# Four pads move every activation tile to one place, 64 bytes short of the weights by 256, in a two-layer decoder trunk

## The chip, the core and the metric

The kernel runs on one core of a Trainium2 chip. The metric is the device time of one execution in microseconds (us). Beside the times of several runs there is one profiled execution, from which the pages and rows below come; its span goes from the first to the last instruction.

## What is computed

Two layers of a decoder with 256 tokens and a width of 1024, all in float32. Each layer adds a token mixer and then a conv-gated MLP to the residual, each behind an rmsnorm, and a last rmsnorm ends it:

```
for i in range(DEPTH):                       # DEPTH = 2
    hn = rms_norm(h, norm_mix[i])
    if kind == 0:   mix = moba_mixer(hn, ...)   # layer 0: causal attention, 16 heads of 64
    elif kind == 1: mix = mla_mixer(hn, ...)    # layer 1: low-rank q and kv latents, shared rotary key
    h = h + mix
    f = conv_ffn(rms_norm(h, norm_ffn[i]), w_gate, conv_w, conv_b, w_up, w_down)
    h = h + f
return rms_norm(h, norm_final)

def conv_ffn(xn, ...):
    g = xn @ w_gate                          # 1024 -> 2816
    gc = conv_b + sum(conv_w[j] * shifted(g, j) for j in range(3))
    return (gelu(gc) * (xn @ w_up)) @ w_down # 2816 -> 1024
```

With 256 tokens the block choice of the first mixer leaves plain causal attention.

## The kernel before

Activations lie with features on the partitions and the 256 tokens along them, as 8 chunks of 128 features (`h`, `zh`, `zl`: 128 x 8 x 256). All weights come as a stream of units in the order in which they are used: `load_unit` sends one DMA of up to 576 KB into `raw` (5 buffers), ScalarE casts it to the rounded format fp32r into `whi` (line 172), and VectorE forms the rest `wlo = raw - whi` (line 173); `whi` and `wlo` have 9 buffers each. Activations are split in the same way, into `zh` and `zl` (lines 184 and 185), `oh` and `ol`, `ch` and `cl`, `hh` and `hl`. A product is then three matmuls, lines 177 to 179 in `mm3`: high by high, high by low, low by high, into one accumulator in PSUM.

In a matmul one operand is loaded into the array first (LDWEIGHTS, PEld in the profile) and the other moves through it (MATMUL, PE). In the profile's `acc<-zh,whi` the first name moves, the second is loaded. The load for the next matmul runs beside the current matmul.

The program goes through these stages, in the order of the code and with no scheduler in between:

1. Layer 0, first head group: Q, K and V from `zh`, `zl` (about 6 to 27 us of the span). Per chunk of features 12 matmuls of Q and K, in which `zh` and `zl` move, alternate with 6 of V, in which weights move and `zh`, `zl` are loaded.
2. Attention of layer 0: head by head, with the products of the next group, and later the output projection (`oh`, `ol` move), filled in between (to about 127 us).
3. The MLP of layer 0, `ffn`: for 22 chunks the gate and the up product (`zh`, `zl` move) and the gate's elementwise work; then the down product in `to_layer1` (`hh`, `hl` move), to about 313 us.
4. Layer 1: the latents (`ch`, `cl`), attention and output projection, to about 410 us; the MLP's gate and up products, to about 534 us; the down product in `to_out`, in which the weights move in pieces of 512 columns and `hh`, `hl` are loaded, to about 598 us; the last norm and the stores.

Tiles are laid one after the other within a pool, and pools one after the other: constants, `rawp`, `wp`, `act` (`h`, `zh`, `zl` and small ones), `sm`, and then one pool that is opened and closed per stage (`at0`, `ff0`, `at1`, `ff1`). All large tiles are whole multiples of 256 bytes per partition, so the first tile of a pool sets the place of all large tiles of it, counted by 256 bytes. Three pads do that in the kernel before: 8 columns (32 bytes) ahead of `act`, 16 columns (64 bytes) in `at0` and `at1`, none in the MLPs.

Of the kernel before, what the change touches and what calls it, by code (L numbers as in the profile page):

```python
# [10 lines left out]
F32 = mybir.dt.float32  # L11
# [5 lines left out]
P = 128  # L17
# [102 lines left out]
def trunk(ctx: ExitStack, tc: tile.TileContext, xT, scalars, gfin, wstream, consts_in, out):  # L120
# [4 lines left out]
    act = ctx.enter_context(tc.tile_pool(name="act", bufs=1))  # L125
    sm = ctx.enter_context(tc.tile_pool(name="sm", bufs=4))
    ps = ctx.enter_context(tc.tile_pool(name="ps", bufs=1, space=PSUM))
    act.tile([P, 8], F32, name="pad")


    zf = rawp.tile([P, UW], F32, name="raw")[:, :S]
# [25 lines left out]
    def load_unit(cuts=2, pieces=1, mid=None):  # L157
        u = state["u"]
        state["u"] += 1
        n = UCOLS[u]  # L160
        raw = rawp.tile([P, UW], F32, name="raw")
        hi = wp.tile([P, UW], F32R, name="whi")
        lo = wp.tile([P, UW], F32R, name="wlo")
        for i in range(pieces):
            a, b = n * i // pieces, n * (i + 1) // pieces
            src = bass.AP(tensor=wstream.tensor, offset=wstream.offset + UOFF[u] + a, ap=[[n, P], [1, b - a]])
            nc.sync.dma_start(raw[:, a:b], src)
            if mid is not None and i == 0:
                mid()
        for i in range(cuts):  # L170
            a, b = n * i // cuts, n * (i + 1) // cuts
            nc.scalar.copy(hi[:, a:b], raw[:, a:b])  # L172
            nc.vector.tensor_sub(lo[:, a:b], raw[:, a:b], hi[:, a:b].bitcast(F32))  # L173
        return hi, lo

    def mm3(o, lh, ll, rh, rl, first, last):
        nc.tensor.matmul(o, lh, rh, start=first, stop=False, skip_group_check=True)  # L177
        nc.tensor.matmul(o, ll, rh, start=False, stop=False, skip_group_check=True)  # L178
        nc.tensor.matmul(o, lh, rl, start=False, stop=last, skip_group_check=True)  # L179
# [31 lines left out]
    def rstd(pc, n):  # L211
        ms = sm.tile([P, NT], F32, name="ms")
        nc.vector.tensor_scalar(ms, pc, 1.0 / n, EPS, op0=ALU.mult, op1=ALU.add)  # L213
        r = sm.tile([P, NT], F32, name="r")
        nc.gpsimd.tensor_tensor(r, ms, mhalf.to_broadcast([P, NT]), op=ALU.pow)  # L215
        return r
# [20 lines left out]
    def rows_sb(r):  # L237
        R = act.tile([P, S], F32, name="R", bufs=2)
        nc.scalar.copy(R, rows(r))
        return R  # L240
# [137 lines left out]

    def ffn(layer, zh, zl, ss):
        with tc.tile_pool(name=f"ff{layer}", bufs=1) as fp:  # L380
            hh = fp.tile([P, FC, S], F32R, name="hh")
            hl = fp.tile([P, FC, S], F32R, name="hl")
            st = {}

            def products(f0, j, pg, pu):
                ug, uu = load_unit(), load_unit()
                runs = ((0, KD),) if f0 + j else ((0, KD - 2), (KD - 2, KD))
                for a, b in runs:
                    for k in range(a, b):
                        for (wh, wl), dst in ((ug, pg), (uu, pu)):  # L390
                            c = slice(k * P, (k + 1) * P)
                            mm3(dst[:, j], wh[:, c], wl[:, c], zh[:, k], zl[:, k], k == 0, k == KD - 1)

            def gate(f0, pg, pu):
                Rb = st["R"][:, None, :].to_broadcast([P, 2, S])
                gm = fp.tile([P, 2, S], F32, name="gm", bufs=2)
                nc.vector.tensor_tensor(gm, pg, Rb, op=ALU.mult)  # L397
                gc = fp.tile([P, 2, S], F32, name="gc", bufs=2)
                for j in range(2):
                    w = cv[:, layer, f0 + j]  # L400
                    nc.scalar.activation(gc[:, j], gm[:, j], AF.Identity, scale=w[:, 2:3], bias=w[:, 3:4])  # L401
                    nc.vector.scalar_tensor_tensor(gc[:, j, 1:], gm[:, j, :S - 1], w[:, 1:2], gc[:, j, 1:],
                                                   op0=ALU.mult, op1=ALU.add)
                    nc.vector.scalar_tensor_tensor(gc[:, j, 2:], gm[:, j, :S - 2], w[:, 0:1], gc[:, j, 2:],
                                                   op0=ALU.mult, op1=ALU.add)
                nc.scalar.activation(gc, gc, AF.Gelu)  # L406
                nc.gpsimd.tensor_tensor(gc, gc, Rb, op=ALU.mult)  # L407
                nc.vector.tensor_tensor(gm, pu, gc, op=ALU.mult)  # L408
                nc.scalar.copy(hh[:, f0:f0 + 2], gm)  # L409
                nc.vector.tensor_sub(hl[:, f0:f0 + 2], gm, hh[:, f0:f0 + 2].bitcast(F32))  # L410

            late = None
            for f0 in range(0, FC, 2):
                pg = ps.tile([P, 2, S], F32, name="acc", bufs=4)
                pu = ps.tile([P, 2, S], F32, name="acc", bufs=4)
                products(f0, 0, pg, pu)
                if late:
                    st["R"] = rows_sb(r)
                    gate(*late)
                    late = None  # L420
                products(f0, 1, pg, pu)
                if f0 == 0:
                    r = rstd(ss.columns(), D)
                    late = (f0, pg, pu)
                else:
                    gate(f0, pg, pu)
            (to_layer1 if layer == 0 else to_out)(fp, hh, hl)
# [87 lines left out]

    zh, zl = new_z()
    with tc.tile_pool(name="at0", bufs=1) as ap:
        ap.tile([P, 16], F32, name="pad")
        oh = ap.tile([P, KD, S], F32R, name="oh")
        ol = ap.tile([P, KD, S], F32R, name="ol")  # L520
        ropeR = ap.tile([P, 2, S], F32, name="ropeR")
# [124 lines left out]
        finish(accs, us, [(oh[:, k], ol[:, k]) for k in (KD - 2, KD - 1)], GF, zh, zl, ss)  # L646

    ffn(0, zh, zl, ss)


    zh, zl = nxt["z"]
    with tc.tile_pool(name="at1", bufs=1) as ap:
        ap.tile([P, 16], F32, name="pad")
        ch = ap.tile([P, CQ + CKV, S], F32R, name="ch")
        cl = ap.tile([P, CQ + CKV, S], F32R, name="cl")
        kTs = [ap.tile([P, HG, S], F32, name=f"kT{i}") for i in range(2)]
# [151 lines left out]
        finish(accs, us, [(oh[:, k], ol[:, k]) for k in (KD - 2, KD - 1)], GF + KD, zh, zl, ss)  # L808

    ffn(1, zh, zl, ss)  # L810


# [25 lines left out]
```

## Time and profile before

| | us |
|---|---|
| median of 3 runs | 606.88 (606.06 to 608.16) |
| the profiled execution | 607.92 |
| its span | 606.1 |
| TensorE busy | 591.7 |
| VectorE busy | 435.2 |
| ScalarE busy | 355.6 |
| GpSimd busy | 63.2 |

Matmuls are pipelined, and the end of one is modelled, so that matmuls overlap in the list and a busy TensorE is not a TensorE at its peak. What can be read exactly is when each one starts. In an unbroken run the distance from start to start is the pace of the engine; it is taken over many matmuls, since starts are shown to 10 ns.

### The profile page before, as it was taken

To read this page: it belongs to the slowest core of one execution; us is meant where nothing else is said; L and a number is where in the kernel's file an instruction comes from. 1 tells how busy PE (TensorE), PEld (TensorE's weight loads), DVE (VectorE), ACT (ScalarE), POOL (GpSimd) and SP (SyncE) were. 2 spreads that over 40 slices of the span, in tenths; PEclk is the share of its full clock that TensorE was granted. 3 is DMA by queue.
4 is the path that set the end of the run, shared out by engine and by line. 5 is a ranking of instruction groups with operands and counts; after the bars stand their busy time and mean duration, and the time that the engine had idled before them with its cause. 6 is when DMAs were issued, how large, how long until landed. Compare 5 with 4: busy or idle time off the path is not lost.

```text
span 606.1 us, 12092 instructions
## 1 busy us (share of the span) xinstructions
PE 591.7 (98%) x4631; PEld 562.9 (93%) x4631; DVE 435.2 (72%) x948; ACT 355.6 (59%) x760; POOL 63.2 (10%) x55
## 2 busy tenths in 40 slices
PE   8999899999999999999999999999999999999994
PEld 8997798999999999999999888999999999988883
DVE  6899878695877777764488889658778777784403
ACT  7687766575655565543366677546666566573302
POOL 1110210000210110200002210000020100110001
PEclk9999999999999999999999999999999999999998
DMA  8746564436466656675637323155466656666101
GB/s 279 279 140 229 166 198 145 142 127 214 146 203 186 199 172 204 186 228 166 187 116 258 127 70 107 70 171 177 140 209 199 195 172 204 200 186 198 40 0 70
DMA packets 30074, 101.62 MB, mean 168 GB/s; under 512 B 3488, under 2 KB 4848, under 8 KB 30016
## 3 DMA queue, kind: packets, MB, share of 16 engines
q1 hardware_dynamic: 29744, 100.24, 51.3%
q8 instruction: 36, 0.59, 0.4%
q0 software_dynamic: 128, 0.35, 0.2%
q10 hardware_dynamic: 144, 0.26, 0.1%
q14 instruction: 22, 0.18, 0.1%
HBM read 99.79 MB, written 1.05 MB: 166 GB/s over the span
## 4 chain that ended last, share of the span: by engine, by line
PE 73%; issue 13%; DVE 6%; DMA 4%; ACT 3%; POOL 1%; SPq 0%; POOLq 0%; DVEq 0%; ACTq 0%
PE acc L177 19%; PE acc L178 18%; PE acc L179 18%; PE sc L274 3%; DMA raw<-in_wstream 3%; PE tr L314 2%; DVE wlo L173 2%; PE sc L179 2%; PE tr L179 2%; PE tr L178 2%; PE sc L178 2%; PE sc L177 2%; PE tr L177 2%; PE sc L300 1%; ACT whi L172 1%
## 5 line engine op out<-in xcount | busy, mean ns | idle before, releaser
L173 DVE TENSOR_TENSOR wlo<-raw,whi 128x512 fp32r<-128x512 f32 (+1 forms) x371 | 240.1, 687 | 61.3 <-ACT whi L172 61.2
L172 ACT CAST whi<-raw 128x512 fp32r<-128x512 f32 (+1 forms) x371 | 210.3, 617 | 119.9 <-PE acc L179 60.1
L177 PE MATMUL acc<-zh,whi 128*128 128x256 f32 x880 | 248.6, 283 | 0.3 <-ACT whi L172 0.3
L178 PE MATMUL acc<-zh,wlo 128*128 128x256 f32 x880 | 246.6, 280 | 0.0
L179 PE MATMUL acc<-zl,whi 128*128 128x256 f32 x880 | 245.8, 280 | 0.0
L177 PEld LDWEIGHTS acc<-zh,whi 128*128 128x128 f32 x880 | 165.6, 189 | 2.9 <-issue 2.0
L178 PEld LDWEIGHTS acc<-zh,wlo 128*128 128x128 f32 x880 | 165.8, 188 | 0.3 <-DVE wlo L173 0.2
L179 PEld LDWEIGHTS acc<-zl,whi 128*128 128x128 f32 x880 | 165.5, 188 | 0.0
L407 POOL TENSOR_TENSOR gc<-gc,R 128x512 f32<-128x512 f32 x22 | 34.9, 1585 | 200.3 <-ACT gc L406 200.3
L409 ACT CAST hh<-gm 128x512 fp32r<-128x512 f32 x22 | 13.7, 621 | 44.1 <-DVE gm L408 44.1
L177 PE MATMUL acc<-oh,whi 128*128 128x256 f32 x128 | 37.8, 295 | 0.0
L178 PE MATMUL acc<-oh,wlo 128*128 128x256 f32 x128 | 36.2, 283 | 0.0
L179 PE MATMUL acc<-ol,whi 128*128 128x256 f32 x128 | 36.0, 281 | 0.0
L288 ACT ACTIVATE pb<-sb,nm 128x128 f32<-128x128 f32 x64 | 28.5, 446 | 7.8 <-DVE nm L285 7.7
L408 DVE TENSOR_TENSOR gm<-acc,gc 128x512 f32<-128x512 f32 x22 | 15.2, 691 | 23.8 <-POOL gc L407 23.8
L215 POOL TENSOR_TENSOR r<-ms,mhalf 128x2 f32<-128x2 f32 x6 | 7.0, 1168 | 190.5 <-DVE ms L213 190.5
L177 PEld LDWEIGHTS acc<-oh,whi 128*128 128x128 f32 x128 | 24.1, 188 | 1.4 <-issue 1.4
L401 ACT ACTIVATE gc<-gm,sc_in 128x256 f32<-128x256 f32 x44 | 24.0, 592 | 1.9 <-DVE gm L397 1.8
L178 PE MATMUL tr<-hh,wlo 128*128 128x256 f32 x88 | 24.6, 280 | 0.0
L177 PE MATMUL sc<-hh,whi 128*128 128x256 f32 x88 | 24.6, 280 | 0.0
L179 PE MATMUL sc<-hl,whi 128*128 128x256 f32 x88 | 24.6, 280 | 0.0
L179 PE MATMUL tr<-hl,whi 128*128 128x256 f32 x88 | 24.6, 280 | 0.0
(150 smaller groups left out, 992.8 us busy)
## 6 DMA issues: line engine op xcount, KB each, us to landing
raw<-in_wstream SPq DMA_DIRECT2D x175, 512.0 KB, 4.2
raw<-in_wstream SPq DMA_DIRECT2D x13, 256.0 KB, 4.7
raw<-in_wstream SPq DMA_DIRECT2D x4, 576.0 KB, 3.8
h<-in_xT SPq DMA_DIRECT2D x8, 128.0 KB, 4.6
gl<-in_gfin SPq DMA_DIRECT2D x1, 512.0 KB, 3.7
out<-hn SPq DMA_DIRECT2D x1, 512.0 KB, 2.6
ropeR<-in_consts POOLq DMA_DIRECT2D x1, 256.0 KB, 4.1
out<-hn ACTq DMA_DIRECT2D x1, 256.0 KB, 3.7
```

Of the source, the lines that this page charges most:

```text
L172: nc.scalar.copy(hi[:, a:b], raw[:, a:b])
L173: nc.vector.tensor_sub(lo[:, a:b], raw[:, a:b], hi[:, a:b].bitcast(F32))
L177: nc.tensor.matmul(o, lh, rh, start=first, stop=False, skip_group_check=True)
L178: nc.tensor.matmul(o, ll, rh, start=False, stop=False, skip_group_check=True)
L179: nc.tensor.matmul(o, lh, rl, start=False, stop=last, skip_group_check=True)
L274: nc.tensor.matmul(o[:, a:b], self.qT(n, t), self.kT(n, b - a), start=True, stop=True)
L288: nc.scalar.activation(pb[:, a:b], sb[:, a:b], AF.Exp, scale=-1.0, bias=nm[:, t:t + 1], accum_out=rs[:, t:t + 1])
L314: nc.tensor.matmul(o[j * HD:(j + 1) * HD, t * P:], self.v(n, t), pT[j][:, a:b], start=t == 0, stop=t == NT - 1)
L401: nc.scalar.activation(gc[:, j], gm[:, j], AF.Identity, scale=w[:, 2:3], bias=w[:, 3:4])
L407: nc.gpsimd.tensor_tensor(gc, gc, Rb, op=ALU.mult)
L408: nc.vector.tensor_tensor(gm, pu, gc, op=ALU.mult)
L409: nc.scalar.copy(hh[:, f0:f0 + 2], gm)
```

## The change

```diff
@@ trunk: pool act
-    act.tile([P, 8], F32, name="pad")
+    act.tile([P, 48], F32, name="pad")
@@ ffn
         with tc.tile_pool(name=f"ff{layer}", bufs=1) as fp:
+            fp.tile([P, 32], F32, name="pad")
             hh = fp.tile([P, FC, S], F32R, name="hh")
@@ pools at0 and at1
-        ap.tile([P, 16], F32, name="pad")
+        ap.tile([P, 32], F32, name="pad")
```

Nothing reads or writes a pad. In the two built programs the instructions, their order on every engine and their waits are the same; what differs is where tiles lie. Bytes into a partition, by 256, with the distance of the activation from the weights in brackets:

| tiles | before | after |
|---|---|---|
| `raw`, `whi`, `wlo` (all buffers) | 32 | 32 |
| `h`, `zh`, `zl`, `R`, `sq`, `ssacc` | 64 (+32) | 224 (-64) |
| `oh`, `ol`, `ch`, `cl`, `qT`, `kT`, `v`, `pn`, `pT` | 0 (-32) | 224 (-64) |
| `hh`, `hl`, `gm`, `gc`, `gl`, `hn` | 192 (+160, or -96) | 224 (-64) |
| constants (`ident`, the mask) | 0 | 0 |

Where the weights move and an activation is loaded, the distance has the other sign.

## Rows read from the trace of the kernel before

**Rows 1.** Busy time of each engine in five stretches, granted clock, DMA share
```profile
core 0: us, PE busy (x) PEld busy (x) DVE busy (x) ACT busy (x) POOL busy (x), PEclk, DMA share, GB/s
30.00:128.00 98.00, 93.92 (x778) 85.56 (x778) 80.57 (x217) 69.64 (x182) 10.80 (x7) 1.00 0.51 167
128.00:251.00 123.00, 123.00 (x1053) 122.84 (x1053) 94.68 (x171) 72.61 (x134) 16.48 (x11) 1.00 0.58 182
251.00:313.00 62.00, 62.00 (x531) 62.00 (x530) 34.85 (x59) 29.09 (x54) 2.03 (x1) 1.00 0.62 191
...
412.00:534.00 122.00, 122.00 (x1045) 121.84 (x1044) 93.84 (x169) 71.74 (x132) 16.46 (x11) 1.00 0.59 186
534.00:599.00 65.00, 64.41 (x290) 51.96 (x288) 27.05 (x46) 22.53 (x43) 2.84 (x3) 1.00 0.30 95
```
**Rows 2.** What TensorE's matmuls waited for: us in total, times, longest
```profile
PE tr L314 <- DVE pT L305: 4.1, 4, 2.2
```
**Rows 3.** Timeline of PE, layer 0 gate and up: first and last of 854 spacings
```profile
151.56 0.28 PE L177 MATMUL acc<-zh,whi 128*128 128x256 f32 x1
...
251.19 0.28 PE L179 MATMUL acc<-zl,whi 128*128 128x256 f32 x1
```
**Rows 4.** Timeline of PE, layer 0 down product: first and last of 524 spacings
```profile
251.66 0.28 PE L177 MATMUL sc<-hh,whi 128*128 128x256 f32 x1
...
313.14 0.28 PE L179 MATMUL tr<-hl,whi 128*128 128x256 f32 x1
```
**Rows 5.** Timeline of PE, layer 1 output projection: first and last of 64 spacings
```profile
402.43 0.28 PE L178 MATMUL acc<-oh,wlo 128*128 128x256 f32 x1
...
410.00 0.28 PE L179 MATMUL acc<-ol,whi 128*128 128x256 f32 x1
```
**Rows 6.** Timeline of PE, V in layer 0: first and last of 21 spacings
```profile
92.54 0.28 PE L178 MATMUL acc<-whi,zl 128*128 128x256 f32 x1
...
95.03 0.28 PE L178 MATMUL acc<-whi,zl 128*128 128x256 f32 x1
```
**Rows 7.** Timeline of PE, layer 1 down product: first and last of 222 spacings
```profile
545.98 0.39 PE L178 MATMUL tr<-whi,hl 128*128 128x512 f32 x1
...
597.78 0.39 PE L178 MATMUL tr<-whi,hl 128*128 128x512 f32 x1
```
**Rows 8.** Timeline of PE, first group of layer 0: first and last of 72 spacings
```profile
11.84 0.28 PE L179 MATMUL acc<-zl,whi 128*128 128x256 f32 x1
...
20.28 0.28 PE L179 MATMUL acc<-zl,whi 128*128 128x256 f32 x1
```
**Rows 9.** Groups of matmuls, one line of three: xcount | busy, mean ns | idle
```profile
L177 PE MATMUL acc<-zh,whi 128*128 128x256 f32 x880 | 248.6, 283 | 0.3 <-ACT whi L172 0.3
L177 PE MATMUL acc<-oh,whi 128*128 128x256 f32 x128 | 37.8, 295 | 0.0
L177 PE MATMUL sc<-hh,whi 128*128 128x256 f32 x88 | 24.6, 280 | 0.0
...
L177 PE MATMUL acc<-whi,zh 128*128 128x256 f32 x64 | 18.7, 293 | 0.0
L177 PE MATMUL sc<-whi,hh 128*128 128x512 f32 x44 | 17.4, 395 | 0.0
```
**Rows 10.** Casts and subtractions with operands at 32 and at 192, all shapes alike
```profile
L173 DVE TENSOR_TENSOR wlo<-raw,whi 128x512 fp32r<-128x512 f32 (+1 forms) x371 | 240.1, 687 | 61.3 <-ACT whi L172 61.2
L172 ACT CAST whi<-raw 128x512 fp32r<-128x512 f32 (+1 forms) x371 | 210.3, 617 | 119.9 <-PE acc L179 60.1
...
L409 ACT CAST hh<-gm 128x512 fp32r<-128x512 f32 x22 | 13.7, 621 | 44.1 <-DVE gm L408 44.1
L410 DVE TENSOR_TENSOR hl<-gm,hh 128x512 fp32r<-128x512 f32 x22 | 15.2, 691 | 11.1 <-ACT hh L409 11.0
```

More of the change, by code (lines that the diff above doesn't have):

```diff
@@ L652, in trunk @@
     with tc.tile_pool(name="at1", bufs=1) as ap:
-        ap.tile([P, 16], F32, name="pad")
+        ap.tile([P, 32], F32, name="pad")
         ch = ap.tile([P, CQ + CKV, S], F32R, name="ch")
```

## The prediction

> **What bounds the kernel now.** The windows by stage come first [rows 1]. From 128 to 251 us and from 412 to 534 us (the gate and up products of the two MLPs) and from 251 to 313 us (the down product of layer 0) TensorE is busy for the whole of each stretch, at a granted clock of 1.00; in the down product of layer 1 for 64.41 of 65 us. In the attention of layer 0 it is still busy for 93.92 of 98 us. VectorE and ScalarE are at 94.68 and 72.61 of 123 us in the same stretch, the DMA at 0.58. The list of waits says the same from the other side: the longest thing TensorE's matmuls waited for is 4.1 us in total, in the attention [rows 2]. So a nanosecond on each product is paid on the path nearly everywhere, and that is the only place where an edit of addresses can be worth much: no instruction, no order and no wait changes.
>
> The question is therefore what sets the pace of one product. All large products are split in three matmuls (lines 177 to 179) and stand back to back, so the pace is the time between two starts, read from the first and the last of a long unbroken run:
> - zh and zl move over weights: 854 spacings from 151.56 to 251.19 us, 116.66 ns [rows 3]. zh and zl lie 32 bytes above the weights by 256: distance +32.
> - hh and hl move over weights: 524 spacings from 251.66 to 313.14 us, 117.33 ns [rows 4]; distance 192 - 32 = 160, or -96.
> - oh and ol move over weights: 64 spacings from 402.43 to 410.00 us, 118.28 ns [rows 5]; distance 0 - 32 = -32.
> - weights move over zh and zl (V of layer 0): 21 spacings from 92.54 to 95.03 us, 118.57 ns, with 10 ns of rounding in 2490 [rows 6]; distance 32 - 64 = -32.
> - weights of 512 columns move over hh and hl: 222 spacings from 545.98 to 597.78 us, 233.33 ns, or 116.67 per 256 columns [rows 7]; distance 32 - 192 = -160, or +96.
>
> Groups 5 and 6 have nothing in common but the distance: another operand moves, in another layer, over other buffers, and the pace is the same. Groups 3 and 5 have all in common but the distance, and differ by 1.62 ns. I take it from this that the distance between what moves and what is loaded, by 256 bytes, sets part of the pace. There is one more point. Where the first group goes from Q and K to V or back, one matmul moves while a weight at its own place is loaded, distance 0. From 11.84 to 20.28 us lie 72 spacings [rows 8]: 44 at +32, 20 at -32 and 8 such. 8440 - 44 x 116.66 - 20 x 118.28 leaves 941 ns, or 117.7 for one; rounding makes that uncertain by about 1 ns.
>
> **The change, part by part.** The weights stay where they are. The pads move h, zh, zl, oh, ol, ch, cl, hh and hl to 224 by 256, so where activations move the distance becomes -64, and where weights move +64. Neither is in the trace, so each is bounded by its neighbours.
>
> *Distance -64.* The nearest rows are -96 with 117.33 [rows 4] and -32 with 118.28 [rows 5]. A straight line between them gives 117.81; the parabola that also takes the point at 0 with 117.7 [rows 8] has its top between them and gives about 118.2. I take 118.0. Counts: the zh and zl groups have three times 880 matmuls, 2640; hh and hl as moving operand three times 88, in sc and in tr each, 528; oh and ol three times 128, 384 [rows 9].
> - zh, zl: 2640 x (118.0 - 116.66) = +3.54 us.
> - hh, hl in layer 0: 528 x (118.0 - 117.33) = +0.35 us.
> - oh, ol: 384 x (118.0 - 118.28) = -0.11 us.
>
> *Distance +64.* The neighbours are +32 with 116.66 [rows 3] and +96 with 116.67 [rows 7]; both ends agree, so I take 116.67.
> - V of layer 0, three times 64 matmuls [rows 9]: 192 x (116.67 - 118.28) = -0.31 us.
> - Down product of layer 1, 44 in each of six groups [rows 9]: 264 x 0 = 0.
>
> The products of the latents in layer 1 (14 of three matmuls in each of four groups by the loops, 168) go from +32 to +64 or from -32 to -64; at the differences above that is under 0.1 us in all. The attention's own matmuls have both operands among the activations, which move together: 0.
>
> *Other engines.* ScalarE and VectorE work on tiles at other places. With all operands at 32 a cast of 512 columns takes 617 ns and a subtraction 687; with all at 192 the same take 621 and 691 [rows 10]. That is 4 ns either way, under work of TensorE that fills the stretch, so 0. The one pair whose distance changes is gc and R in POOL's product (from 128 to 0); POOL is busy 16.48 of 123 us [rows 1], and the two PSUM pairs behind it cover it. The DMA that lands h now writes to 224 instead of 64. Every transfer of weights lands at 32 already, so a place off 64 bytes is no hindrance that shows: I count 0, and bound it by 0.3 us either way, for the eight loads of x and the stores at the end, which nothing covers.
>
> *Sum:* 3.54 + 0.35 - 0.11 - 0.31 = +3.5 us. It is made against the profiled execution: 607.92 us with a span of 606.1, where the 1.8 us around the span stay. The median before is 606.88, 1.04 below the profiled one, and a change of pace shifts both alike: 606.9 + 3.5 = 610.4 us. With the straight line's 117.81 the sum is 3.04 + 0.25 - 0.18 - 0.31 = +2.8, and with 118.28 for all of it 4.28 + 0.50 - 0.31 = +4.5: 609.7 to 611.4. Of the 2640, some 500 lie in the attention and the latents, where a slower product could hide in a wait; 4.08 us of idle time in 98 [rows 1] say that few do, and if all did, 0.7 us would go.
>
> The rows show that the same matmul takes 116.66 or 118.28 ns by where its operands lie. The Trainium skill, page "TensorE: Matmul & The Clock Gate", section "Step-by-step: what each phase is for", says that TensorE has two independent read ports to SBUF, one for the moving operand and one for the weight load, so that loading the next weights takes nothing from the running matmul. By that rule the place of a tile could not matter, and the sum would be 0 instead of +3.5. The trace speaks against it in rows 3 and 5, as long as it is the distance that makes them differ; if it is something else in those stages, the rule holds, and its result is the second rival.
>
> **The rivals.** *Faster: -64 is better than anything in the trace.* All five long runs have a distance that is an odd multiple of 32 bytes; -64 is a multiple of 64, and if the loss comes where two reads are out of step within a piece of 64 bytes, the neighbours say nothing. For it: no run shows such a distance for long. Against it: the eight overlaps at distance 0, also a multiple of 64, came to 117.7, in the middle of the others. Price: as far below the best pace seen as the best is below the worst, 1.6 ns, gives 115.0: 2640 x -1.66 - 528 x 2.33 - 384 x 3.28 - 0.31 = -4.4 - 1.2 - 1.3 - 0.3 = -7.2, or 599.7 us. It decides as soon as the pace at -64 is below about 116.5. Chance 0.26.
>
> *No change.* Either the place has no part in the pace (606.9 us), or -64 is as good as +32: then zh and zl stay, hh and oh gain 528 x 0.67 + 384 x 1.62 = 1.0 us and V 0.3, 605.6 us. For the first: the stages differ in more than the distance, in how they go round PSUM. Against it: groups 5 and 6. Chance 0.20.
>
> *Slower than the worst pace seen.* -64 is the top of the curve, and it is higher than both neighbours: at 119.0 it is 6.18 + 0.88 + 0.28 - 0.31 = +7.0, or 613.9 us. For it: the point at 0 is lower than the one at -32, so a top lies somewhere between -96 and 0. Chance 0.08.
>
> **How the numbers follow.** The forecast, 609.7 to 611.4 with 610.4 in the middle, has 0.46. This kernel's runs tell from no change what is more than about 0.3%, or 1.8 us: the limits are 605.1 and 608.7. Slower is the forecast and the last rival, 0.54; within 0.3% is the second, 0.20; faster is the first, 0.26. The range leaves out the half of the first rival that lies furthest down and most of the last: 601 to 612.5.
>
> **What would show it.** In the profile after, the run from about 151 us should have its 854 spacings at 117.8 to 118.3 ns instead of 116.66, hh at the same pace instead of 117.33, oh at the same pace instead of 118.28, V and the down product of layer 1 at 116.67 per 256 columns. All products of one direction should have one pace, since all have one distance. The stretches of the two gate and up products should each grow by about 1.4 us, and TensorE should be as busy in them as before. I am wrong if the paces by stage stay as they are (then the distance is not the cause), or if the pace at -64 lies outside of its two neighbours.

## The result and the profile after

| us | before | after |
|---|---|---|
| median | 607.41 of 4 runs (606.06 to 608.16) | 598.81 of 4 runs (596.47 to 603.31) |
| profiled execution, its span | 607.92, 606.1 | 603.31, 601.5 |

The ratio of the times is 0.988, with an interval from 0.984 to 0.991. The change makes the kernel faster, by about 1.2%, where the prediction said 3.5 us slower. The times of after also lie over 6.8 us, those of before over 2.1. Ratios and intervals, here and below, leave out executions more than 1.5% above the quickest of their kernel, which takes the slowest 3 of 7 out of again and 4 of 10 out of shift64, while the medians are of all executions.

Busy time by stretch, after; the columns are those of [rows 1]:
```profile
128.00:251.00 123.00, 123.00 (x1045) 122.84 (x1044) 93.69 (x169) 71.64 (x132) 16.46 (x11) 1.00 0.58 184
...
412.00:534.00 122.00, 122.00 (x1057) 121.31 (x1056) 96.33 (x175) 74.53 (x138) 16.43 (x11) 1.00 0.61 192
```
TensorE is busy without a gap in both gate and up stretches, as before, at a granted clock of 1.00. But the profile has 1045 matmuls in the first stretch, where it had 1053, and 1057 in the second, where it had 1045: one layer became slower and the other quicker.

Timeline of PE, after: first and last of the 854 spacings in layer 0, the same in layer 1, and first and last of the 222 spacings of 512 columns (columns: start, length, engine, line, operation, out<-moving,loaded):
```profile
150.08 0.28 PE L177 MATMUL acc<-zh,whi 128*128 128x256 f32 x1
...
250.66 0.28 PE L179 MATMUL acc<-zl,whi 128*128 128x256 f32 x1
...
434.03 0.28 PE L177 MATMUL acc<-zh,whi 128*128 128x256 f32 x1
...
530.82 0.28 PE L179 MATMUL acc<-zl,whi 128*128 128x256 f32 x1
...
542.32 0.39 PE L178 MATMUL tr<-whi,hl 128*128 128x512 f32 x1
...
593.13 0.39 PE L178 MATMUL tr<-whi,hl 128*128 128x512 f32 x1
```
Layer 0: 100.58 us over 854 is 117.78 ns. Layer 1: 96.79 over 854 is 113.33. Both runs have the same operands in the same places at the same distance, -64; [rows 3] had 116.66. The down product of layer 1 went from 233.33 [rows 7] to 228.89 ns. Every other unbroken run of 37 spacings or more at -64 in this trace has one of the same two paces. (A list of starts lacks a record here and there, so spacings are counted from the program.) So there is a slow one, 117.78, close to the 118.0 of the forecast, and a quick one, 113.33, which no row of before showed.

Of the 4.6 us of span, layer 1's gate and up run gives 2.85 and the 512-wide run 0.99; layer 0's run takes 0.95 more than [rows 3], the down product of layer 0 0.2 more than [rows 4]. The rest, some 1.9 us, comes from the attention and the shorter runs.

The other engines did not move (groups of after, as [rows 10]; hh and hl at their new place took 622 and 691 ns):
```profile
L173 DVE TENSOR_TENSOR wlo<-raw,whi 128x512 fp32r<-128x512 f32 x363 | 234.5, 685 | 60.1 <-ACT whi L172 60.0
L172 ACT CAST whi<-raw 128x512 fp32r<-128x512 f32 x363 | 205.4, 617 | 116.0 <-PE acc L179 58.1 <-PE tr L179 25.7 <-PE tr L178 16.5
```

### The profile page after: what moved, and what is told of

Read it like the earlier page. It is cut to its first block, busy times and chain, and to the rows that moved or that the text cites. A ratio compares the mean times of both kernels' runs of the same rounds, so it can differ in the third digit from the quotient of the medians.

```text
span 601.5 us, 12092 instructions
## 1 busy us (share of the span) xinstructions
PE 586.3 (97%) x4631; PEld 558.5 (93%) x4631; DVE 435.8 (72%) x948; ACT 356.1 (59%) x760; POOL 61.3 (10%) x55
## 4 chain that ended last, share of the span: by engine, by line
PE 75%; issue 12%; DVE 5%; ACT 2%; DMA 2%; POOL 2%; SPq 0%; POOLq 0%; DVEq 0%; ACTq 0%
PE acc L177 19%; PE acc L178 19%; PE acc L179 19%; PE sc L274 3%; DMA raw<-in_wstream 2%; PE tr L314 2%; PE tr L177 2%; PE sc L177 2%; PE sc L179 2%; PE tr L179 2%; PE tr L178 2%; PE sc L178 2%; PE sc L300 1%; DVE wlo L173 1%; DVE rt L531 1%
## 5 line engine op out<-in xcount | busy, mean ns | idle before, releaser
L178 PE MATMUL sc<-hh,wlo 128*128 128x256 f32 x88 | 24.7, 281 | 0.0
L177 PE MATMUL tr<-hh,whi 128*128 128x256 f32 x88 | 24.7, 281 | 0.0
```

## The experiments

Theory *distance*: the distance between the moving and the loaded operand by 256 bytes alone sets the pace, and -64 simply is a good value. Rivals: the place in memory counts and not the distance; other engines' accesses count; or something of the stage counts. A second question came with the result: what picks between the two paces at -64?

**again.** The changed kernel once more, without an edit, in more runs.

> The changed kernel once more, unchanged. In its first profile every long run of products kept one of two paces, 113.33 or 117.78 ns from start to start, and never a third (layer 0 gate and up 117.79 over 1454 spacings, layer 1 gate and up 113.33 over 854). Theory A, two lockings at distance -64, picked anew at each start: the same two paces and no other, but in some runs of products swapped against the first profile; times of single executions spread over several us, between about 594 (all long runs at 113.33) and 608 (all at 117.78). Theory B, the pace belongs to the place in the program (layer 1 is quick, layer 0 slow): every run of products keeps the pace of the first profile, and times differ by under 2 us.

Median 601.87 us of 7 runs: 596.87, 597.63, 600.51, 601.87, 606.43, 606.79, 607.22; ratio 0.990 (0.986 to 0.994), and 0.991 by the medians of all. Timeline of PE in the execution of 596.87: first and last of layer 0's gate and up run, its down product, layer 1's gate and up run:
```profile
150.18 0.28 PE L177 MATMUL acc<-zh,whi 128*128 128x256 f32 x1
...
246.97 0.28 PE L179 MATMUL acc<-zl,whi 128*128 128x256 f32 x1
...
247.42 0.28 PE L177 MATMUL sc<-hh,whi 128*128 128x256 f32 x1
...
306.81 0.28 PE L179 MATMUL tr<-hl,whi 128*128 128x256 f32 x1
...
427.59 0.28 PE L177 MATMUL acc<-zh,whi 128*128 128x256 f32 x1
...
524.38 0.28 PE L179 MATMUL acc<-zl,whi 128*128 128x256 f32 x1
```
854, 524 and 854 spacings, all of 113.33 ns. So one kernel has both paces in the same run of products, in different executions. In layer 0 the run goes over into the down product and the latents without a break, and all of it keeps one pace: (854 + 524 + 68) x 4.45 = 6.4 us; in layer 1 it is 854 x 4.45 = 3.8 us. Neither, one or both slow gives four times, 596.9 and 3.8, 6.4 and 10.2 us more: 596.9, 600.7, 603.3 and 607.1. The times of after and again lie near these, and each profiled execution agrees: after, with layer 0 slow alone, took 603.31 us, this one, with neither, 596.87.

**d0, d128, d_p64.** All activations at distance 0, at 128 and at +64, by the lengths of the same pads alone.

> All activations at distance 0 from the weights by 256 (no pad in act, 32 columns in the others, everything at 32). Theory A with 'multiples of 64 can lock at 113.33': two paces again, 113.33 and a slower one, time 594 to 608 us. Theory C, -64 alone is special and 0 is the mean of its neighbours: one pace of about 117.7 everywhere, about 609 to 611 us.

> All activations 128 bytes from the weights by 256, as far as can be. Theory A with 'any multiple of 64': 113.33 among the paces, 594 to 608 us. Theory C: between its neighbours +96 (116.67) and -96 (117.33), about 117.0, 606 to 608 us. If two reads at half the period never meet, below 113.33 everywhere, under 592 us.

> All activations 64 bytes above the weights by 256 (act pad 16 columns, the others 32): the mirror of the change. Theory A: two paces, 113.33 and 117.78, where activations move, and the same two where weights move (now at -64); 594 to 608 us. Theory C (-64 alone): where activations move one pace near that at +32, 116.7, about 605 us; the down product of layer 1, now at -64, at 229 ns per 512 columns or more.

| kernel | us (range) | ratio (interval) | zh, hh in layer 0, ns | 512 columns, ns |
|---|---|---|---|---|
| d0 | 613.89 (612.92 to 614.54) | 1.010 (1.008 to 1.012) | 120.0 | 226.77 |
| d128 | 611.51 (611.23 to 612.82) | 1.007 (1.005 to 1.009) | 118.66 | 232.34 |
| d_p64 | 609.31 (608.38 to 610.27) | 1.003 (1.002 to 1.004) | 117.78 | 233.33 |

Timeline of PE, d0: first and last of 854 spacings of zh and zl, and of 222 spacings of 512 columns; then the 854 spacings of d_p64:
```profile
151.66 0.28 PE L177 MATMUL acc<-zh,whi 128*128 128x256 f32 x1
...
254.14 0.28 PE L179 MATMUL acc<-zl,whi 128*128 128x256 f32 x1
...
553.99 0.39 PE L178 MATMUL tr<-whi,hl 128*128 128x512 f32 x1
...
604.33 0.39 PE L178 MATMUL tr<-whi,hl 128*128 128x512 f32 x1
```
```profile
150.76 0.28 PE L177 MATMUL acc<-zh,whi 128*128 128x256 f32 x1
...
251.34 0.28 PE L179 MATMUL acc<-zl,whi 128*128 128x256 f32 x1
```
Distance 0 is the slowest place for 256 columns, 120.0 ns, and the quickest for 512. At +64 all long runs of 256 columns stood at 117.78, and all ten executions within 1.9 us. Neither theory held for 0 or for 128: there was no 113.33, and no pace that lies between those of the neighbours. At +64 the single 116.7 fell, and the quick pace of the other theory stood in no long run, only in short ones (21 spacings of zh and zl at 113.33, from 87.0 us).

**bench16, bench8.** Products alone, without the network and without work of other engines, at each distance in steps of 16 and of 8 bytes; operands are made once, ahead. Each bench ran once. bench16 goes four times through its 16 places; STEPS is 16 and STEP 4 columns, so 16 bytes, and `small` makes 42 matmuls:
```diff
+    for rep in range(4):
+        for o in range(STEPS):
+            small(o * STEP, 14)
+            gap(rep + 1)
```

> A bench, not the network: it leaves out everything but products. Two weight tiles at a fixed place, two activation tiles that are read from 16 places, 0 to 240 bytes above the weights by 256 in steps of 16; at each place 42 matmuls of 256 columns in threes as in the kernel, four times over, with one to four small matmuls as a break between; then 24 matmuls of 512 columns per place in which the weights move. Theory A (the distance by 256 alone sets which paces there are): 120.0 at 0, 116.67 at 32, 113.33 or 117.78 at 64 and at 192, 118.66 at 128, 117.33 at 160, 118.3 at 224, the same in all four repetitions except at 64 and 192, and 512 columns at 226.8 for 0, 233.3 at 160 (weights 96 above). Theory D (the stage or what the other engines do sets the pace): one pace at all places, since nothing else runs here. What lies between, at odd multiples of 16, is not known: a pace under 113.33 there would point to a better layout.

> A bench like the first, products alone and no network: 32 places, 0 to 248 bytes above the weights by 256 in steps of 8, 30 matmuls of 256 columns at each, and this time a break ahead of every place: in the first pass four small matmuls, in the second one of 256 columns, in the third one small, in the fourth two small; then 512 columns with the weights moving, in steps of 16. Theory A with two lockings: at 64 and 192 some passes give 113.33 and others 117.78, by the break ahead; everywhere else the four passes give one pace, that of the first bench (120.0 at 0, 116.7 at 32, 118.6 at 128, 117.3 at 160, 118.4 at 224). Theory F (the 113.33 of the first bench at 112 and 192 came only from the place it was entered from): 112 falls in two as well. A place at which all four passes give 113.33 or less would be the better layout.

The small matmuls of `gap` (L151) did not break anything in bench16: all of them stand ahead of the first place, up to 93 us, so each place was entered from its neighbour, and the four passes are alike. In bench8 the breaks stand where the code has them.

Timeline of PE, bench16: first and last of 32 spacings at 112, at -64 and at 0:
```profile
131.20 0.28 PE L155 MATMUL acc<-zh,whi 128*128 128x256 f32 x1
...
134.83 0.28 PE L157 MATMUL acc<-zl,whi 128*128 128x256 f32 x1
...
155.88 0.28 PE L155 MATMUL acc<-zh,whi 128*128 128x256 f32 x1
...
159.51 0.28 PE L157 MATMUL acc<-zl,whi 128*128 128x256 f32 x1
...
175.58 0.28 PE L155 MATMUL acc<-zh,whi 128*128 128x256 f32 x1
...
179.42 0.28 PE L157 MATMUL acc<-zl,whi 128*128 128x256 f32 x1
```
3.63 us over 32 is 113.4, 3.84 over 32 is 120.0. Paces over the four passes, ns, good to about 0.3:

| distance | 0 | 16 | 32 | 48 | 64 | 80 | 96 | 112 | 128 | -112 | -96 | -80 | -64 | -48 | -32 | -16 |
|---|---|---|---|---|---|---|---|---|---|---|---|---|---|---|---|---|
| pace | 120.0 | 118.8 | 116.7 | 118.3 | 117.8 | 119.9 | 119.9 | 113.3 | 118.6 | 118.6 | 117.3 | 119.2 | 113.3 | 119.0 | 118.4 | 117.2 |

In bench8 the odd multiples of 8 stood at about 120 nearly everywhere, 112 at 113.3 behind some ten slower spacings, and 32, 64, -64 and 128 as above. Two distances had two paces there: 16 stood at 116.65 behind the break of one matmul of 256 columns and at 113.35 behind the other three, against 118.8 in bench16; -96 at 117.3 behind that same break and at 118.6 behind the others. So a break picks between paces at some distances; but -64 was at 113.3 in all eight passes, and its slow pace has been seen in the network alone. The distances that the network has agree with bench16: 116.7 at 32, 117.3 at -96, 118.4 at -32 [rows 3 to 5]. So the dependence on the distance needs no other engine, and the pace jumps between neighbours 16 bytes apart; no curve goes through these points. The Trainium skill, page "TensorE: Matmul & The Clock Gate", section "Step-by-step: what each phase is for", says that TensorE has two independent SBUF read ports, one for the moving operand and one for the weight load, and that loading the next weights takes no read bandwidth from the running matmul. The bench does not agree with it: products alone take 113.4 or 120.0 ns by their places, at a granted clock of 0.999 over the whole run.

**shift64.** Everything, weights and activations, 64 bytes further on; the distance stays -64.
```diff
+    const.tile([P, 16], F32, name="pad0")
```

> The changed kernel with everything moved up by 64 bytes, weights too (a pad of 16 columns ahead of all pools): the weights at 96 by 256, activations at 32, the distance -64 as before. Theory A (distance): the two paces 113.33 and 117.78, time 594 to 608 us. Theory E (the place 224 itself, or the weights at 32): another set of paces, and a time outside of that or back at 606 to 608 us with the paces of before.

602.3 us of 10 runs (596.28 to 607.88), ratio 0.989 (0.987 to 0.992), and 0.992 by the medians of all. Timeline of PE, its 854 spacings in layer 0 and in layer 1:
```profile
151.21 0.28 PE L178 MATMUL acc<-zh,whi 128*128 128x256 f32 x1
...
247.99 0.28 PE L180 MATMUL acc<-zl,whi 128*128 128x256 f32 x1
...
428.69 0.28 PE L178 MATMUL acc<-zh,whi 128*128 128x256 f32 x1
...
529.27 0.28 PE L180 MATMUL acc<-zl,whi 128*128 128x256 f32 x1
```
Layer 0 is at 113.33, layer 1 at 117.78: both paces again, in the other order. The distance counts, not the place. In the 21 executions of after, again and shift64, 5 lie from 596.2 to 597.7 us, 9 from 600.5 to 603.4 and 7 from 606.0 to 607.9.

**act_only, rest_only.** Half of the change each: in act_only the pad of `act` alone (the other pads adjusted so that oh, ch and hh stay at their old places), in rest_only the other three.

> Only h, zh, zl and the small tiles of their pool go to 224 (distance -64); oh, ol, ch, cl stay at 0 and hh, hl at 192 by pads that make up for the shift. Theory A: gate and up products and Q, K at 113.33 or 117.78; hh 117.33, oh 118.3, down product of layer 1 233.3 as before. 2640 x (-3.33 to +1.11) ns: 598 to 610 us, spread over executions.

> Only oh, ol, ch, cl, hh, hl and their stages go to 224; h, zh, zl stay at 64 (distance +32). Theory A: gate, up, Q, K at 116.67 as before; hh 113.33 or 117.78; oh the same two; the down product of layer 1 at 228.9 per 512 columns instead of 233.3 (264 x -4.4 = -1.2 us). Together -1.2 - (0.1 to 1.5) + (0.2 or -2.1): 603 to 607 us.

act_only: 600.79 us of 4 runs (600.59 to 601.86), ratio 0.990 (0.988 to 0.991). Both gate and up runs at 113.33, the rest at the paces of before. rest_only: 603.06 us of 4 (602.84 to 603.55), ratio 0.993 (0.992 to 0.995). Timeline of PE, act_only's 854 spacings in layer 0, then rest_only's 854 and its 524 of hh and hl:
```profile
150.47 0.28 PE L177 MATMUL acc<-zh,whi 128*128 128x256 f32 x1
...
247.26 0.28 PE L179 MATMUL acc<-zl,whi 128*128 128x256 f32 x1
```
```profile
150.24 0.28 PE L177 MATMUL acc<-zh,whi 128*128 128x256 f32 x1
...
249.88 0.28 PE L179 MATMUL acc<-zl,whi 128*128 128x256 f32 x1
250.34 0.28 PE L177 MATMUL sc<-hh,whi 128*128 128x256 f32 x1
...
309.73 0.28 PE L179 MATMUL tr<-hl,whi 128*128 128x256 f32 x1
```
zh at -64: 96.79 us instead of 99.63; in rest_only zh stays at 116.67 and hh is at 113.33 (59.39 us for 524). Each half moves the products whose operand it moves, and no others. Against the kernel before of the same runs, 607.17 us, the halves gain 6.4 and 4.1; together that is 596.7, which the quickest executions of the changed kernel have. Neither half spread in its four runs, where a spread was expected of act_only.

**relock, relock_best.** Both put a break into each gate and up run, one small matmul ahead of chunk 6; relock_best also lays hh and hl of layer 1 at distance 0, where 512 columns were quickest.
```diff
+                if f0 == 6:
+                    nc.tensor.matmul(pg[:, 0, 0:2], ones, ones[:, :2], start=True, stop=True)
-            fp.tile([P, 32], F32, name="pad")
+            fp.tile([P, (32, 48)[layer]], F32, name="pad")      # relock_best alone
```

> The changed kernel with one small matmul (two columns, ones by ones, into an accumulator that the next product overwrites) ahead of the fourth pair of chunks in each MLP, about 11 us into the long run of gate and up products and behind the last place at which a weight came late (149.5 and 433.5 us in the changed kernel's profile). In the bench a break of small matmuls at distance -64 was followed by 113.3 ns in all four passes. Theory A with 'a late weight leaves the run in either locking, a small break leaves it in the quick one': behind the break 113.33 in both layers in the profile, and every execution between 595.5 and 598.5 us, 596.9 in the middle (the quickest execution of the changed kernel took 596.3; the two breaks cost 0.3 us each). Theory G (the locking is picked at random at any break): executions spread from 596 to 608 us as before, median 600 to 603.

> The same, and in layer 1 the pad of the MLP is 48 columns instead of 32, so that hh and hl lie at the place of the weights by 256 there (distance 0), where 512 columns took 226.8 ns with all tiles at distance 0 and 226.7 in the bench, against 228.9 at 64. Expected against the kernel with the small matmuls alone: 264 x -2.1 ns = -0.6 us, 596.3 us in the middle. If the wide matmuls' pace depends on more than the distance, no difference.

relock: 599.63 us of 8 runs (596.54 to 605.42). relock_best: 604.0 of 6 (595.61 to 607.98). Timeline of PE, relock_best in layer 1: a run from 433.54 to 444.02 us, the break (L418), and the run behind it:
```profile
433.54 0.28 PE L178 MATMUL acc<-zh,wlo 128*128 128x256 f32 x1
...
444.02 0.28 PE L179 MATMUL acc<-zl,whi 128*128 128x256 f32 x1
...
444.16 0.25 PE L418 MATMUL acc<-ones 128*128 128x2 f32 x1
...
444.48 0.28 PE L178 MATMUL acc<-zh,wlo 128*128 128x256 f32 x1
...
534.34 0.28 PE L179 MATMUL acc<-zl,whi 128*128 128x256 f32 x1
```
10.48 us over 89 before the break and 89.86 over 763 behind it are both 117.8: such a break keeps the pace that was there. The other three long runs of the two profiles agree: 117.8 on both sides in layer 0 here, 113.3 on both sides in both layers of relock. The execution of relock_best with both runs slow took 606.72 us, near the 607.1 above. The theory that a small matmul leaves the quick pace behind it fell. The 512-wide products were at 226.77, as expected of distance 0.

**fix0.** Ten matmuls at distance 0, of which no second pace has been seen, ahead of chunk 6.
```diff
+                if f0 == 6 and j == 0:
+                    for _ in range(10):
+                        nc.tensor.matmul(pg[:, 0], ug[0][:, :P], ug[0][:, :S], start=True, stop=True, skip_group_check=True)
```

> The changed kernel with one addition: in each MLP, at the first product of chunk 6 (about 161 and 445 us), ten extra matmuls over a weight tile that is also the loaded operand, distance 0, ahead of the products. Their result is overwritten. In the bench, places of pace 120.0 stood ahead of the places at -64, and these were at 113.33 each time. Theory 'phase': a stretch at 120.0 leaves the two reads in one fixed relation, from which -64 always goes to its quick pace. Then the products behind the ten matmuls stand at 113.33 in both layers in every execution; the ten cost 1.2 us a layer, so all executions are between 598 and 600.5 us, with none above 602. Rival 'chance': what is ahead doesn't matter, or not in this way; then one layer or both stand at 117.78 in some executions, and the times spread from 599 to 609 us as those of the changed kernel do, 2.4 higher.

(In bench16 the place ahead of -64 was at 119.2, in bench8 at 120.0.) Six runs: 598.54, 598.92, 598.98, 599.07, 599.78 and 603.82; ratio 0.988 (0.985 to 0.990). The profiled one is that of 603.82. Timeline of PE: 764 spacings behind the ten in layer 0, 764 in layer 1:
```profile
162.28 0.28 PE L177 MATMUL acc<-zh,whi 128*128 128x256 f32 x1
...
248.86 0.28 PE L179 MATMUL acc<-zl,whi 128*128 128x256 f32 x1
...
441.32 0.28 PE L177 MATMUL acc<-zh,whi 128*128 128x256 f32 x1
...
531.30 0.28 PE L179 MATMUL acc<-zl,whi 128*128 128x256 f32 x1
```
113.3 in layer 0, where the run ahead of the ten was at 113.35 too, and 117.8 in layer 1, where it was at 117.78: in this execution the ten changed nothing. The other five lie where the theory had all six, but behind the ten the slow pace can stand as well, so the theory fell. Whether the ten make the quick pace more frequent, six executions don't show.

**z112.** zh and zl at 112, the quick place of the benches that is no multiple of 64; oh, ch and hh stay at -64.
```diff
-    act.tile([P, 48], F32, name="pad")
+    act.tile([P, 24], F32, name="pad")
-        return act.tile([P, KD, S], F32R, name="zh"), act.tile([P, KD, S], F32R, name="zl")
+        zh = act.tile([P, KD * S + 64], F32R, name="zh")
+        zl = act.tile([P, KD * S + 64], F32R, name="zl")
+        return tuple(t[:, 4:4 + KD * S].rearrange("p (k s) -> p k s", s=S) for t in (zh, zl))
-            fp.tile([P, 32], F32, name="pad")
+            fp.tile([P, 56], F32, name="pad")
-        ap.tile([P, 32], F32, name="pad")      # at0 and at1
+        ap.tile([P, 56], F32, name="pad")
```

> Only zh and zl lie elsewhere than in the changed kernel: 112 bytes above the weights by 256 instead of 64 short (pads of the other pools are longer by the same, so oh, ch and hh stay at -64; h, R and sq lie at 128). In both benches 112 stood at 113.33 or 114.0, never at 117.8. Theory 'one pace at 112': both gate and up runs at 113.3 to 114.0 in every execution; the down product of layer 0 stays at -64, so it may be at either of its paces: times of 596.5 to 601 us. Rival 'two paces here too': the benches entered 112 in one way only; then runs of 854 at some other pace appear and the times spread to 605 or more, as those of the changed kernel.

595.79 us of 5 runs (595.18 to 596.32), ratio 0.981 (0.980 to 0.983). Timeline of PE, the 854 spacings in layer 0 and in layer 1:
```profile
149.22 0.28 PE L177 MATMUL acc<-zh,whi 128*128 128x256 f32 x1
...
246.03 0.28 PE L179 MATMUL acc<-zl,whi 128*128 128x256 f32 x1
...
426.14 0.28 PE L177 MATMUL acc<-zh,whi 128*128 128x256 f32 x1
...
522.94 0.28 PE L179 MATMUL acc<-zl,whi 128*128 128x256 f32 x1
```
Both runs are at 113.35, the down product of layer 0 behind the first at 113.33, and the five times lie within 1.2 us. V, whose weights now move at -112, is at about 120 instead of 118.2, and the kernel still has the lowest median of all that ran: it is 1.9% below before, and its slowest execution is as quick as the quickest of after. That all five executions were quick is what 'one pace at 112' expected; five executions don't exclude a rare second one.

## Why the prediction was wrong, step by step

- *What bounds the kernel.* Right. TensorE is busy through the same stretches, the other engines and their waits stayed, and the time went with the pace of the products alone.
- *The distance by 256 sets the pace.* Right as to which paces there are: shift64 moved everything and found the same two, and the benches show the dependence with no other engine at work. It does not settle which of them a run takes.
- *Distance -64 bounded by its neighbours.* This is the step that failed. The prediction drew a line and a parabola through -96, -32 and 0 and took 118.0. Measured was 113.33 or 117.78; the quick one is 4.0 below the one neighbour and 5.0 below the other, which is what the prediction had named as its sign of being wrong. That the slow one lies 0.2 from the 118.0 is luck. Nothing bounds a place by its neighbours: bench16 goes 119.2, 113.3, 119.0 in steps of 16 bytes. The terms of the sum that hang on it should read, with the quick pace throughout: zh and zl 2640 x -3.33 = -8.8 instead of +3.54, hh 528 x -4.0 = -2.1 instead of +0.35. With the slow pace throughout they are 2640 x 1.12 = +3.0 and +0.2. No execution was all of one kind: even where both long runs are slow, as in the profile of relock_best, the shorter runs of zh and zl are partly quick, and with the gain at +64, below, the slowest execution of again, 607.22, is no slower than before.
- *The pace at 0 from eight single overlaps* [rows 8]. Wrong: 117.7 was read, a run at 0 has 120.0. The eight stood singly between products at +32 and -32, and single spacings do not show the pace of a run: in that stretch they go from 113 to 123 ns. They served as the argument against the rival that came true, so the misreading weighed against the right sign.
- *Distance +64 taken at 116.67, since both neighbours had it.* Wrong by the same step. Besides, the neighbour at +96 was half of a product of 512 columns; at 96 one of 256 columns takes 119.9 in bench16. The 512-wide products went to 228.89: 264 x -4.44 = -1.2 us instead of 0. V was at 117.8 or 113.33.
- *Other engines and DMA at 0.* Right: casts 617, subtractions 685 ns, and hh and hl at 622 and 691 from their new place.
- *One pace for all products of one direction.* Wrong: two. The trace of before had shown as much at +32, in a run of 51 spacings just ahead of [rows 3], behind a matmul of the norm (L234); they are the first two rows below. That run is at 117.78, [rows 3] with the same operands at 116.66.
- *The rivals.* "-64 is better than anything in the trace" came true, with 599.7 as its time; its point of decision, a pace below 116.5, was the right one. That its time is so near is luck: it had 115.0 for every product, a pace that no long run has, and the median hangs on how many executions are slow (601.87 in again). Its reason was not: 0 and 128 are multiples of 64 and slow, 112 is none and quick. The range began at 601.0, since half of that rival was cut off as too far down; the median lies 2.2 below it. No change and the slower rival fell.

What picks between two paces is known in part: the rows point to what stands ahead of the run, as bench8 does at 16. Timeline of PE, first and last of 51 spacings behind L234 in before; then, in after, of 46 behind the two small matmuls of the norm (L208), and of 51 behind L234:
```profile
144.79 0.28 PE L178 MATMUL acc<-zh,wlo 128*128 128x256 f32 x1
...
150.80 0.28 PE L178 MATMUL acc<-zh,wlo 128*128 128x256 f32 x1
```
```profile
137.44 0.28 PE L178 MATMUL acc<-zh,wlo 128*128 128x256 f32 x1
...
142.66 0.28 PE L179 MATMUL acc<-zl,whi 128*128 128x256 f32 x1
...
143.32 0.28 PE L178 MATMUL acc<-zh,wlo 128*128 128x256 f32 x1
...
149.32 0.28 PE L178 MATMUL acc<-zh,wlo 128*128 128x256 f32 x1
```
That is 117.78, 113.35 and 117.78 ns. In both layers of all seven profiled executions with zh at -64 (after, again, shift64, act_only, relock, relock_best, fix0) the run behind L208 is quick and the one behind L234 slow; these never change.

What stays open: why one way in leaves the quick pace and another the slow one, and what picks it for the long runs, which do change. Both long runs begin behind a weight that came late, and the rows there look alike in slow and quick executions (after at 149.85 and 150.08 us, again at 149.95 and 150.18: 0.23 us both), so it is less than these rows resolve. Why act_only's four executions were all quick, and why d_p64's ten were all slow, isn't settled either.

## What to carry to other kernels

Where TensorE is the bound and its loads run beside its matmuls, the place of the moving operand against the loaded one, by 256 bytes, was worth up to 6.7 ns in 120 here, more than 5%, for products of 256 columns; measure the table of paces with a small kernel of products alone, and don't interpolate it. Then look at the spread of the executions: a place that was quick in every execution (112 here) beats one that is quick in some only. A pace is read from long unbroken runs, never from single matmuls between others.

## What the runs showed that was not expected

- One program with the same operands in the same places has two paces, 113.33 or 117.78 ns a product, each kept over up to some 1450 products, through changes of buffers and through a small matmul in between. It spreads the time of one kernel over 11 us.
- Moves of 16 bytes change the pace by up to 6.6 ns (96: 119.9, 112: 113.3), and in bench8 nearly all distances that are odd multiples of 8 bytes cost about 120.
- What is worst for products of 256 columns can be best for those of 512: distance 0 has 120.0 and 226.77, which is 113.4 per 256 columns.
